# A ConvFFN up-projection computed as seven half-size products per column tile, with the weight sums of the down-projection made earlier in the program

## The chip, the cores and the metric

One core of one Trainium2 chip runs one decoder layer in one launch. The metric is the device time of one execution in microseconds (us), less is better. The kernel before takes 1924.64 us (median of three runs, 1924.29 to 1924.65).

## What is computed

The layer is a sliding-window attention followed by a gated MLP, both with RMSNorms around them, for 512 tokens of width 2048 in float32. The part that matters here:

```python
def conv_ffn(h, w_up, conv_w, w_down):
    u = h @ w_up                                   # (512, 2048) @ (2048, 11264)
    c = conv_w[0] * up[:, 0:S] + ...               # causal, width 3, per column
    gate, val = jnp.split(c, 2, axis=-1)
    return (jax.nn.silu(gate) * val) @ w_down      # (512, 5632) @ (5632, 2048)
```

## The kernel before, in words

**Arithmetic.** Every float32 operand is split into a high and a low half of type fp32r: `split` (L61) lets ScalarE (ACT) write the high half and VectorE (DVE) the difference, and `prod` (L79) issues three matmuls, high by high, high by low, low by high. The activations live as `ah` and `al`, [128 partitions, 4 token blocks, 16 row blocks, 128 tokens]. `weights` (L65) loads a 512 KB weight block into `raw`, and splits it into a pair of a ring of eight (`wh`, `wl`, pool `wsp`).

**Stages.** Attention and its projections; the output projection `oproj` (L466, column groups d = 0 to 3, the last one written out token block by token block); `finish_tok` (L435), which for a token block b makes the residual sum, the RMSNorm, and in `xt` the normalized tokens, that `turn_tok` (L456) transposes on TensorE (PE) into `ah`, `al`; the up-projection; the down-projection.

**Up-projection.** The 11264 columns are handled as 44 column tiles f, each with a gate and a value half of 128 columns. Tiles 0 and 1 are computed in `up_part` (L496) in two sweeps of 256 tokens, since the later tokens come last. For the other 42, `up` (L540) runs `project` (L97) twice: 2 halves by 16 row blocks by 3 matmuls of 512 tokens, 96 matmuls in all. `gate` (L528) then applies convolution, SiLU and product, and its last line stores the tile to DRAM (`hd`, L534).

**Down-projection.** It is already computed with seven instead of eight half-size products (`product`, L608), on 2 token halves (m) by 2 halves of the rows (par). The `hd` parts are read back as four tiles `hq` (m, par); tile (1, 0) lies in a pool of its own (`early`), so that `fetch` (L513) can bring it in while the up-projection runs. The sums of weight blocks that these products need are made by `weight_sums` (L547): one 2 MB load of four blocks by SyncE (SP), four DVE additions (L551), one 2 MB store to a table `td` in DRAM, issued by GpSimd (POOL). It is called after every second tile f, 22 times. `weight_form` (L595) reads blocks from the table or the original weights.

**What sets the order.** The program is written in one stream; a scheduler of the framework places the instructions of ACT, DVE, SP and POOL in a fixed order for each engine. Matmuls keep the order of the program. Each engine runs its list strictly in order, and an instruction that waits holds up all that stand behind it. The same holds for the DMA issues of SP and POOL.

Of the kernel before, what the change touches and what calls it, by code (L numbers as in the profile page):

```python
# [41 lines left out]
def trunk(ctx, tc, xT, x, grow, table, onehot, masked, sinks, conv,  # L42
# [82 lines left out]
    with ExitStack() as att:  # L125
# [10 lines left out]
        with ExitStack() as ph:  # L136
# [26 lines left out]
            for kt in range(KT):  # L163
                if kt == 0:
                    for h in range(2):
                        r = first[:, KT:] if h == 0 else pa.tile([P, 512], F32, name="xs")
                        c = KT + h * S
                        nc.sync.dma_start(r if h else first, xT[:, c if h else 0:c + S])
                        if h == 0:
                            w = [wsp.tile([P, 1024], F32R, name=n) for n in ("wh", "wl")]  # L170
# [243 lines left out]
    hd = dr.tile([2, 2, P, NP, HALF], F32, name="hd")  # L414
    td = dr.tile([NP, P, 4, 1024], F32, name="td")

    with ExitStack() as op:
        acc = op.enter_context(pool("acc", 1, side="right"))
        y = acc.tile([P, NT, D], F32, name="y")
        gp = op.enter_context(pool("gp", 1))  # L420
# [84 lines left out]
        up_part(2)  # L505


    early = ctx.enter_context(pool("early", 1, side="right"))
    fap = ctx.enter_context(pool("fap", 2, side="right"))
    hq = {(1, 0): early.tile([P, NP, HALF], F32, name="hq10")}  # L510
    batches = [(g, min(g + GB, NP)) for g in range(0, NP, GB)]

    def fetch(m, par, g0, g1):  # L513
        nc.sync.dma_start(hq[m, par][:, g0:g1, :], hd[m, par, :, g0:g1, :])  # L514

    with ExitStack() as us:
# [11 lines left out]
        def gate(f, o):  # L528
            cg = conv_half(o[0], f, 0)
            nc.scalar.activation(cg, cg, AF.Silu)  # L530
            cv = conv_half(o[1], f, 1)
            nc.vector.tensor_tensor(cv, cg, cv, ALU.mult)
            kp, par = divmod(f, 2)
            nc.sync.dma_start(hd[:, par, :, kp, :].rearrange("m p t -> p m t"),  # L534
                              cv.rearrange("p (m t) -> p m t", m=2))
            for g0, g1 in batches:
                if par == 0 and kp == g1 - 1:
                    fetch(1, 0, g0, g1)

        def up(f):  # L540
            o = [bank(k) for k in ((0, 1), (2, 5))[f % 2]]
# [5 lines left out]
        def weight_sums(kp):  # L547
            t = tsp.tile([P, 4, 1024], F32, name="ts")
            nc.sync.dma_start(t, wdn[4 * kp:4 * kp + 4].rearrange("q p n -> p q n"))
            for o, a, b in ((2, 0, 2), (0, 0, 1), (1, 2, 1), (3, 1, 3)):  # L550
                nc.vector.tensor_tensor(t[:, o, :], t[:, a, :], t[:, b, :], ALU.add)  # L551
            nc.gpsimd.dma_start(td[kp], t)

        gate(0, o[0:2])
        gate(1, o[2:4])
# [7 lines left out]
    acts.close()  # L563
    acc = ctx.enter_context(pool("acc2", 1))
    y = acc.tile([P, NT, D], F32, name="y")
    g3 = acc.tile([P, D], F32, name="g3")
    rest = ctx.enter_context(pool("rest", 1))
    raws = (wraw, ctx.enter_context(pool("wraw2", 2)))
    for m, par in ((0, 1), (1, 1)):
        hq[m, par] = rest.tile([P, NP, HALF], F32, name=f"hq{m}{par}")  # L570
    small = ctx.enter_context(pool("small3", 4))
    last = ctx.enter_context(ExitStack())
    hq[0, 0] = last.enter_context(pool("hq00", 1)).tile([P, NP, HALF], F32, name="hq00")
# [5 lines left out]
    XB, ZB = (3, 4, 6, 7), (0, 1, 2, 5)  # L579

    def act_form(first, second, sign, g0, g1):
        n = g1 - g0
        a = hq[first][:, g0:g1, :]
        hi = wsp.tile([P, 1024], F32R, name="wh")[:, :n * HALF].rearrange("p (k t) -> p k t", t=HALF)
        lo = wsp.tile([P, 1024], F32R, name="wl")[:, :n * HALF].rearrange("p (k t) -> p k t", t=HALF)
        if second is None:
            nc.scalar.activation(hi, a, AF.Copy, scale=-1.0)
            nc.vector.scalar_tensor_tensor(lo, a, -1.0, hi.bitcast(F32), ALU.mult, ALU.subtract)
        else:
            t = fap.tile([P, GB, HALF], F32, name="fa")[:, :n, :]  # L590
            nc.vector.tensor_tensor(t, a, hq[second][:, g0:g1, :], ALU.subtract if sign < 0 else ALU.add)
            split(hi, lo, t)
        return hi, lo

    def weight_form(src, kp):  # L595
        raw = raws[kp % 2].tile([P, 1024], F32, name="raw")
        table, q = src
        nc.sync.dma_start(raw, td[kp, :, q, :] if table else wdn[4 * kp + q])
        hi = wsp.tile([P, 1024], F32R, name="wh")
        lo = wsp.tile([P, 1024], F32R, name="wl")  # L600
        split(hi, lo, raw)
        return hi, lo

# [152 lines left out]
```

## Time and profile before

| | |
|---|---|
| median of three runs | 1924.64 us |
| profiled execution, its own time | 1924.01 us |
| span in the profile, first to last instruction | 1922.0 us |
| PE busy | 1909.6 us (99%) |
| DVE busy | 1114.5 us (58%) |
| ACT busy | 788.5 us (41%) |
| moved by DMA | 374.78 MB, mean 195 GB/s |

The span is divided by what runs: attention and its projections up to about 373 us, the output projection with `finish_tok` to 528 us, tiles 0 and 1 of the up-projection to 577 us, the other 42 tiles to 1492 us, then the down-projection. "Busy" counts the time in which at least one instruction of the engine is under way; matmuls overlap, so their pace is read from start to start, not from their durations. In lists of instructions a row gives start, duration, engine, line, operation, and in brackets the idle time ahead of it with what ended it.

### The profile page before, as it was taken

How to read it: one execution, taken by the hardware profiler on the slowest of the kernel's cores; microseconds unless marked ns; L12 is line 12 of the kernel's file. 1: busy time of each engine (PE TensorE's matmuls, PEld its weight loads, DVE VectorE, ACT ScalarE, POOL GpSimd, SP SyncE). 2: the span in 40 equal slices, each digit the busy share in tenths (PEclk: the TensorE clock that was granted, in tenths of full speed). 3: DMA queues.
4: the chain of work that ended last, by engine and by line, in shares of the span. 5: the costliest groups of instructions: out<-in, count | busy, mean ns of one | idle time of the engine just before them, and what ended most of it. 6: DMA issues, size and time to landing. Idle time of an engine off the chain costs nothing.

```text
span 1922.0 us, 22964 instructions
## 1 busy us (share of the span) xinstructions
PE 1909.6 (99%) x8846; PEld 1589.2 (83%) x8846; DVE 1114.5 (58%) x1655; ACT 788.5 (41%) x1236; POOL 14.3 (1%) x30
## 2 busy tenths in 40 slices
PE   9999999999999999999999999999999999999998
PEld 7888888888898888888888888888888888888886
DVE  5468888723675555565555533334343476666885
ACT  6357777622443222222222222222222355545553
POOL 0000000000000000000000000000000000000000
PEclk9999999999999999999999999999999999999999
DMA  8623235352367787787778633333332965665773
GB/s 310 149 97 107 92 107 174 135 189 96 119 229 284 286 300 275 283 301 295 285 289 307 234 111 105 121 109 113 118 107 91 352 227 188 195 228 199 246 235 110
DMA packets 105644, 374.78 MB, mean 195 GB/s; under 512 B 10592, under 2 KB 24128, under 8 KB 100800
## 3 DMA queue, kind: packets, MB, share of 16 engines
q1 hardware_dynamic: 98336, 317.98, 48.1%
q0 software_dynamic: 3168, 46.14, 6.5%
q10 hardware_dynamic: 4032, 9.21, 1.5%
q8 instruction: 69, 1.13, 0.2%
q14 instruction: 39, 0.32, 0.1%
HBM read 300.90 MB, written 72.39 MB: 194 GB/s over the span
## 4 chain that ended last, share of the span: by engine, by line
PE 97%; DMA 2%; DVE 0%; ACT 0%; issue 0%; DVEq 0%; SPq 0%; ACTq 0%
PE b L74 96%; PE b L77 2%; DMA hq<-hd 1%; DMA hd<-c 1%; DMA raw<-td 0%; DMA first<-in_xT 0%; DVE x L652 0%; DVE wl L63 0%; ACT wh L62 0%; ACT ah L157 0%; ACT junk L641 0%; DVE y L643 0%; DVEq L752 0%; SPq L514 0%; DVE rs L111 0%
## 5 line engine op out<-in xcount | busy, mean ns | idle before, releaser
L63 DVE TENSOR_TENSOR wl<-raw,wh 128x1024 fp32r<-128x1024 f32 (+1 forms) x411 | 498.5, 1220 | 610.3 <-ACT wh L62 609.4
L62 ACT ACTIVATE wh<-raw 128x1024 fp32r<-128x1024 f32 (+1 forms) x411 | 431.2, 1057 | 818.5 <-PE b L74 675.1
L74 PE MATMUL b<-ah,wh 128*128 128x512 f32 (+1 forms) x1792 | 691.1, 386 | 0.2 <-ACT wh L62 0.2
L74 PE MATMUL b<-ah,wl 128*128 128x512 f32 (+1 forms) x1792 | 684.9, 382 | 0.1
L74 PE MATMUL b<-al,wh 128*128 128x512 f32 (+1 forms) x1792 | 684.0, 382 | 0.0
L74 PEld LDWEIGHTS b<-ah,wl 128*128 128x128 f32 x1792 | 336.8, 188 | 66.0 <-DVE wl L63 0.4
L74 PEld LDWEIGHTS b<-ah,wh 128*128 128x128 f32 x1792 | 337.2, 188 | 63.2 <-ACT wh L62 1.7
L74 PEld LDWEIGHTS b<-al,wh 128*128 128x128 f32 x1792 | 337.3, 188 | 61.5
L74 PE MATMUL b<-wl,wh 128*128 128x512 f32 x616 | 239.8, 389 | 0.8 <-DVE wl L63 0.8
L74 PE MATMUL b<-wh 128*128 128x512 f32 x616 | 239.8, 389 | 0.1
L74 PE MATMUL b<-wh,wl 128*128 128x512 f32 x616 | 239.7, 389 | 0.0
L74 PEld LDWEIGHTS b<-wl,wh 128*128 128x128 f32 x616 | 115.7, 188 | 24.9 <-DVE wl L63 1.1
L74 PEld LDWEIGHTS b<-wh 128*128 128x128 f32 x616 | 115.7, 188 | 24.5 <-ACT wh L62 0.6
L74 PEld LDWEIGHTS b<-wh,wl 128*128 128x128 f32 x616 | 115.7, 188 | 24.0
L74 PE MATMUL b<-wh,ah 128*128 128x512 f32 x320 | 126.5, 395 | 0.0
L74 PE MATMUL b<-wh,al 128*128 128x512 f32 x320 | 124.8, 390 | 0.0
L74 PE MATMUL b<-wl,ah 128*128 128x512 f32 x320 | 124.6, 389 | 0.0
L551 DVE TENSOR_TENSOR ts<-ts 128x1024 f32<-128x1024 f32 x88 | 107.4, 1221 | 27.9 <-DMA ts<-in_wdn 26.7
L524 DVE SCALAR_TENSOR_TENSOR c<-b,cw,c 128x511 f32<-128x511 f32 x88 | 65.4, 744 | 22.9 <-ACT c L523 22.9
L523 ACT ACTIVATE c<-b,cw 128x512 f32<-128x512 f32 x88 | 59.1, 671 | 43.3 <-PE b L74 43.3
L74 PEld LDWEIGHTS b<-wh,al 128*128 128x128 f32 x320 | 60.1, 188 | 12.9
L74 PEld LDWEIGHTS b<-wl,ah 128*128 128x128 f32 x320 | 60.2, 188 | 11.7
(108 smaller groups left out, 1142.9 us busy)
## 6 DMA issues: line engine op xcount, KB each, us to landing
raw<-in_wup SPq DMA_DIRECT2D x176, 512.0 KB, 3.6
ts<-in_wdn SPq DMA_DIRECT2D x22, 2048.0 KB, 8.3
td<-ts POOLq DMA_DIRECT2D x22, 2048.0 KB, 7.8
raw<-td SPq DMA_DIRECT2D x88, 512.0 KB, 4.9
raw<-in_wdn SPq DMA_DIRECT2D x66, 512.0 KB, 4.4
raw<-in_wq SPq DMA_DIRECT2D x32, 512.0 KB, 3.4
raw<-in_wo SPq DMA_DIRECT2D x32, 512.0 KB, 3.4
hd<-c SPq DMA_DIRECT2D x44, 256.0 KB, 3.4
```

The costliest lines, as they stand in the source:

```text
L62: nc.scalar.activation(hi, src, AF.Copy)
L63: nc.vector.tensor_tensor(lo, src, hi.bitcast(F32), ALU.subtract)
L74: tc.keep_in_program_order(nc.tensor.matmul(o, l, r, start=start, stop=stop, skip_group_check=more))
L77: tc.keep_in_program_order(nc.tensor.transpose(o, src, ident))
L523: nc.scalar.activation(c, o, AF.Copy, scale=w[:, 2:3])
L524: nc.vector.scalar_tensor_tensor(c[:, 1:], o[:, :S - 1], w[:, 1:2], c[:, 1:], ALU.mult, ALU.add)
L551: nc.vector.tensor_tensor(t[:, o, :], t[:, a, :], t[:, b, :], ALU.add)
```

## The change

Four things are done.

1. **Seven products.** Tiles f = 4 to 43 go to `up_pair`: gate and value half are taken as two column blocks, the 2048 rows as two row blocks, the 512 tokens as two halves, and the 2 by 2 by 2 product is computed with seven products of 256 tokens by 8 row blocks (Winograd's form). The sums of token blocks are made once, in `token_sums` and `settle`: three forms get tiles of their own, two overwrite quarters of `ah` and `al`, two are quarters as they stand. The sums of weight blocks are made for each tile: four DVE additions, then seven splits in place of four. Partial results are read out of PSUM by four ACT copies (`shot` and one more) and three DVE subtractions of 256 columns. Tile 2 stays as before; tile 3 is computed in two sweeps of 256 tokens (`up_by_tokens`), after each of which a quarter of `ah`, `al` is overwritten.
2. **Weight sums.** `weight_sums` now works block by block on three 512 KB buffers: four loads and four stores of 512 KB, all issued by POOL. Six of its 22 calls stand in the output projection, one ahead of tile 3, fifteen are spread over tiles 5 to 40.
3. **Space.** The ring of weight halves is five instead of eight during the up-projection.
4. **Read-back.** `hq` (1, 0) has no early place any more: all four `hq` tiles are fetched after the up-projection.

```diff
     def weights(dram, u):
...
-        hi = wsp.tile([P, 1024], F32R, name="wh")
-        lo = wsp.tile([P, 1024], F32R, name="wl")
+        hi, lo = halves()
...
+    def weight_sums(kp, sums):
+        def load(q):
+            t = sums.tile([P, 1024], F32, name="ts")
+            nc.gpsimd.dma_start(t, wdn[4 * kp + q])
+            return t
+        def add(q, t, other):
+            nc.vector.tensor_tensor(t, t, other, ALU.add)
+            nc.gpsimd.dma_start(td[kp, :, q, :], t)
+        b11, b21 = load(0), load(2)
+        add(2, b21, b11)
+        b12 = load(1)
+        add(0, b11, b12)
+        add(1, b12, b21)
+        b22 = load(3)
+        add(3, b22, b12)
...
+                if u % 3 == 2:
+                    weight_sums(2 * (d - 1) + u // 3, sums)
...
+                if b < 2 and kt == 8:
+                    weight_sums(4 + b, sums)
...
+        def times(o, n, w, fresh):
+            o3 = o[:, :HALF].rearrange("p (a b) -> p a b", a=2)
+            a = forms[n]
+            for k in range(8):
+                prod(o3, cols(w, k), tuple(v[:, :, k, :] for v in a), fresh and k == 0, k == 7, not fresh)
...
+        def up_pair(f):
+            X, Y, Z = (bank(k) for k in ((0, 1, 6), (3, 4, 7))[f % 2])
...
+            nc.vector.tensor_tensor(t, b11, b21, ALU.add)
+            times(X, 2, form(t), True)
+            s1 = shot(X, "s1")
+            b12 = block(f, 0, 1)
+            times(Z, 7, form(b12), True)
+            s7 = shot(Z, "s7")
+            nc.vector.tensor_tensor(t, t, b12, ALU.add)
+            times(X, 5, form(t), False)
+            s2 = shot(X, "s2")
+            nc.vector.tensor_tensor(b11, b11, b12, ALU.add)
+            times(Z, 6, form(b11), False)
+            b22 = block(f, 1, 1)
+            nc.vector.tensor_tensor(t, t, b22, ALU.add)
+            times(X, 3, form(t), False)
+            s3 = shot(X, "s3")
+            nc.vector.tensor_tensor(ug[:, :HALF], Z[:, :HALF], s2, ALU.subtract)
+            times(Y, 1, form(b21), True)
+            nc.vector.tensor_tensor(uv[:, :HALF], s3, s7, ALU.subtract)
+            times(X, 4, form(b22), False)
+            nc.vector.tensor_tensor(ug[:, HALF:], s1, Y[:, :HALF], ALU.subtract)
+            nc.scalar.activation(uv[:, HALF:], X[:, :HALF], AF.Copy, scale=-1.0)
+            gate(f, (ug, uv))
-        for f in range(2, NF):
-            up(f)
-            if f % 2 == 0:
-                weight_sums(f // 2 - 1)
-        weight_sums(NP - 1)
+        for f in range(4, NF):
+            up_pair(f)
+            if f % 5 in (0, 2) and 7 + 2 * (f // 5 - 1) + (f % 5) // 2 < NP:
+                weight_sums(7 + 2 * (f // 5 - 1) + (f % 5) // 2, sums)
...
-    for q in ((0, 0), (0, 1), (1, 1)):
+    for q in ((1, 0), (0, 0), (0, 1), (1, 1)):
         for g0, g1 in batches:
             fetch(*q, g0, g1)
```

The change moves instructions in three places that the prediction speaks of.

**Place 1, DVE in the up-projection.** Before, one tile f with one set of weight sums (`ts`) in it; `wl` is the low half of a weight block, `c0` and `c1` the convolution, numbers are those of the buffers:

```order
L63 TENSOR_TENSOR wl_7293<-raw_7290,wh_7292 128x1024
L63 TENSOR_TENSOR wl_7323<-raw_7320,wh_7322 128x1024
L524 SCALAR_TENSOR_TENSOR c0_7136<-b0_7014,cw_80,c0_7136 128x511
L525 SCALAR_TENSOR_TENSOR c0_7136<-b0_7014,cw_80,c0_7136 128x510
L551 TENSOR_TENSOR ts_8787<-ts_8787 128x1024 x2
L63 TENSOR_TENSOR wl_7353<-raw_7350,wh_7352 128x1024
L551 TENSOR_TENSOR ts_8787<-ts_8787 128x1024 x2
L63 TENSOR_TENSOR wl_7383<-raw_7380,wh_7382 128x1024
L524 SCALAR_TENSOR_TENSOR c1_7141<-b1_7015,cw_80,c1_7141 128x511
L525 SCALAR_TENSOR_TENSOR c1_7141<-b1_7015,cw_80,c1_7141 128x510
L532 TENSOR_TENSOR c1_7141<-c0_7136,c1_7141 128x512
L63 TENSOR_TENSOR wl_7433<-raw_7430,wh_7432 128x1024
```

Now, from the second addition of one set to its fourth, within one tile of the bunch (`raw` and `bw` are sums of weight blocks and the blocks themselves, `ug`, `uv` the results of a tile):

```order
L433 TENSOR_TENSOR ts_13699<-ts_13699,ts_13705 128x1024
L674 TENSOR_TENSOR raw_9093<-bw_9089,bw_9091 128x1024
L65 TENSOR_TENSOR wl_8922<-raw_8856,wh_8921 128x1024
L433 TENSOR_TENSOR ts_13705<-ts_13705,ts_13701 128x1024
L65 TENSOR_TENSOR wl_8953<-bw_8852,wh_8952 128x1024
L562 SCALAR_TENSOR_TENSOR c1_8825<-uv_8598,cw_83,c1_8825 128x511
L683 TENSOR_TENSOR bw_9089<-bw_9089,bw_9125 128x1024
L562 SCALAR_TENSOR_TENSOR c0_8820<-ug_8597,cw_83,c0_8820 128x511
L686 TENSOR_TENSOR raw_8856<-raw_8856,bw_8980 128x1024
L563 SCALAR_TENSOR_TENSOR c1_8825<-uv_8598,cw_83,c1_8825 128x510
L433 TENSOR_TENSOR ts_13711<-ts_13711,ts_13705 128x1024
L563 SCALAR_TENSOR_TENSOR c0_8820<-ug_8597,cw_83,c0_8820 128x510
```

What moved: the sums of the tile's own blocks (L674 to L686) stand between its splits (L65), and the four additions of a set (L433) are spread between them. The calls are written two in five tiles, but the list has one set in every tile from the fifth on, 54 additions in 14 tiles in a row, and none behind them.

**Place 2, SP at the end of the up-projection.** Before, the last rows that bring in weight blocks for the down-projection (`raw`), the last tiles' stores (`hd`), and the four `hq` (numbered by the buffer: 5346 is (1, 0), 11135 is (0, 1), 11136 is (1, 1), 11143 is (0, 0)):

```order
L598 DMA raw<-td 128x1024 x3
L534 DMA hd<-c_10967 128x2x256
L514 DMA hq_5346<-hd 128x512
L598 DMA raw<-td 128x1024 x2
L514 DMA hq_11135<-hd 128x1024 x5
L514 DMA hq_11136<-hd 128x1024 x4
L534 DMA hd<-c_11108 128x2x256
L514 DMA hq_11136<-hd 128x1024
L598 DMA raw<-td 128x1024 x4
L514 DMA hq_11143<-hd 128x1024 x5
L514 DMA hq_11143<-hd 128x512
L514 DMA hq_11135<-hd 128x512
```

Now (15675 is (0, 0), 15663 is (1, 0), 15667 is (0, 1), 15668 is (1, 1)):

```order
L744 DMA raw<-td 128x1024 x2
L548 DMA hq_15675<-hd 128x1024 x2
L572 DMA hd<-c_15637 128x2x256
L548 DMA hq_15675<-hd 128x1024 x3
L548 DMA hq_15675<-hd 128x512
L548 DMA hq_15663<-hd 128x1024 x5
L548 DMA hq_15663<-hd 128x512
L548 DMA hq_15667<-hd 128x1024 x5
L548 DMA hq_15667<-hd 128x512
L548 DMA hq_15668<-hd 128x1024 x5
L548 DMA hq_15668<-hd 128x512
L744 DMA raw<-td 128x1024 x18
```

What moved: all of `hq` (1, 0) stands behind the store of the very last tile and behind four fetches of (0, 0), and the fifth weight block of the down-projection stands behind all four `hq`.

**Place 3, DVE in `finish_tok` of the first token block.** Before:

```order
L437 TENSOR_REDUCE s_4516<-ssm 128x1
L108 TENSOR_SCALAR rs<-s_4516 128x1
L110 RECIPROCAL rs<-rs 128x1
L111 SCALAR_TENSOR_TENSOR rs<-rs 128x1
L112 TENSOR_SCALAR rs<-rs 128x1
L113 TENSOR_TENSOR s_4516<-rs 128x1
L444 SCALAR_TENSOR_TENSOR y<-y,s_4516,xt 128x1024 x2
L447 TENSOR_TENSOR s_4527<-s_4527 128x1
L108 TENSOR_SCALAR rs<-s_4527 128x1
```

Now:

```order
L465 TENSOR_REDUCE s_4602<-ssm 128x1
L433 TENSOR_TENSOR ts<-ts 128x1024
L117 TENSOR_SCALAR rs<-s_4602 128x1
L119 RECIPROCAL rs<-rs 128x1
L433 TENSOR_TENSOR ts<-ts 128x1024
L120 SCALAR_TENSOR_TENSOR rs<-rs 128x1
L433 TENSOR_TENSOR ts<-ts 128x1024
L121 TENSOR_SCALAR rs<-rs 128x1
L122 TENSOR_TENSOR s_4602<-rs 128x1
L472 SCALAR_TENSOR_TENSOR y<-y,s_4602,xt 128x1024 x2
L475 TENSOR_TENSOR s_4613<-s_4613 128x1
L117 TENSOR_SCALAR rs<-s_4613 128x1
```

What moved: three additions of a set of weight sums (L433) stand ahead of the residual sum (L472), and behind these rows a fourth stands ahead of the normalized tokens `xt`.

## Rows read from the trace of the kernel before

**Rows 1.** The page, chain that ended last: shares of the span by engine.

```profile
PE 97%; DMA 2%; DVE 0%; ACT 0%; issue 0%; DVEq 0%; SPq 0%; ACTq 0%
```

**Rows 2.** Busy times by stretch: start:end, length, PE, PEld, DVE, ACT, POOL, PEclk, DMA, GB/s.

```profile
577.00:1493.00 916.00, 916.00 (x4047) 758.91 (x4046) 451.06 (x464) 255.88 (x298) 11.18 (x21) 1.00 0.59 211
1493.00:1922.00 429.00, 418.52 (x1845) 345.79 (x1843) 287.22 (x284) 210.00 (x238) 0.00 (x0) 0.99 0.65 221
1905.00:1922.00 17.00, 7.41 (x33) 5.82 (x31) 9.02 (x21) 2.47 (x8) 0.00 (x0) 0.85 0.33 123
```

**Rows 3.** PE's waits, whole span: sum in us, times, longest.

```profile
PE b L74 <- DVE zero L140: 1.5, 1, 1.5
PE b L74 <- DVE wl L63: 0.8, 1, 0.8
```

**Rows 4.** Timeline of PE from 640 us, 512 columns: first and last of 90 matmuls.

```profile
639.67 0.39 PE L74 MATMUL b<-ah,wl 128*128 128x512 f32 x1
...
659.84 0.39 PE L74 MATMUL b<-al,wh 128*128 128x512 f32 x1
```

**Rows 5.** Timeline of PE from 560 us, 256 columns: first and last of 144 matmuls.

```profile
559.75 0.28 PE L74 MATMUL b<-al,wh 128*128 128x256 f32 x1
...
576.91 0.28 PE L74 MATMUL b<-ah,wh 128*128 128x256 f32 x1
```

**Rows 6.** Timeline of DVE, a stretch in which it runs without idle time.

```profile
568.92 1.22 DVE L63 TENSOR_TENSOR wl<-raw,wh 128x1024 fp32r<-128x1024 f32 x1
570.06 0.74 DVE L524 SCALAR_TENSOR_TENSOR c<-b,cw,c 128x511 f32<-128x511 f32 x1
570.72 1.21 DVE L551 TENSOR_TENSOR ts<-ts 128x1024 f32<-128x1024 f32 x1
571.85 0.74 DVE L525 SCALAR_TENSOR_TENSOR c<-b,cw,c 128x510 f32<-128x510 f32 x1
...
574.30 0.68 DVE L532 TENSOR_TENSOR c<-c,c 128x512 f32<-128x512 f32 x1
574.90 1.22 DVE L63 TENSOR_TENSOR wl<-raw,wh 128x1024 fp32r<-128x1024 f32 x1
```

**Rows 7.** Groups of instructions by line and shape: the nearest to a 256-column subtraction.

```profile
L217 DVE TENSOR_TENSOR vs<-qn,vs 128x256 fp32r<-128x256 f32 x8 | 2.9, 416 | 0.0
```

**Rows 8.** Timeline of DVE and POOL, last addition of two sets and their stores.

```profile
572.61 0.67 POOL L552 DMA_DIRECT2D td<-ts  x1 [569.57 <-DVE c L525]
...
596.05 1.22 DVE L551 TENSOR_TENSOR ts<-ts 128x1024 f32<-128x1024 f32 x1
...
597.58 0.53 POOL L552 DMA_DIRECT2D td<-ts  x1 [24.30 <-DVE ts L551]
```

**Rows 9.** DMA issues from 600 to 1050 us: count, KB each, median us to landing.

```profile
DMA packets 30997, 130.58 MB, mean 290 GB/s; under 512 B 2336, under 2 KB 7712, under 8 KB 28576
...
raw<-in_wup SPq DMA_DIRECT2D x84, 512.0 KB, 5.5
...
hq<-hd SPq DMA_DIRECT2D x3, 512.0 KB, 3.9
```

**Rows 10.** The same from 1120 to 1480 us, where no weight sums are made.

```profile
DMA packets 14469, 40.24 MB, mean 112 GB/s; under 512 B 1360, under 2 KB 5712, under 8 KB 14452
...
raw<-in_wup SPq DMA_DIRECT2D x59, 512.0 KB, 3.4
```

**Rows 11.** Timeline of DVE and PE, end of finish_tok for the first token block.

```profile
500.54 2.74 DVE L451 SCALAR_TENSOR_TENSOR xt<-y,s,g 128x512 f32<-128x512 f32 x4
...
504.99 0.60 PE L77 MATMUL b<-ident,xt 128*128 128x128 f32 x4
```

**Rows 12.** Timeline of SP and ACT at the start of the down-projection.

```profile
1492.13 7.22 SPq L514 DMA_DIRECT2D hq<-hd  x9
...
1514.23 1.06 ACT L62 ACTIVATE wh<-raw 128x1024 fp32r<-128x1024 f32 x1 [0.24 <-DMA raw<-td]
...
1515.52 1.06 ACT L62 ACTIVATE wh<-raw 128x1024 fp32r<-128x1024 f32 x1 [0.23 <-DMA raw<-td]
```

More of the change, by code (lines that the diff above doesn't have):

```diff
@@ L53, in trunk @@
     act = acts.enter_context(pool("act", 1))
+    more = acts.enter_context(ExitStack())
+    ring = {"slots": [wsp] * 5 + [more.enter_context(pool("wsp2", 3))] * 3, "next": 0}
     def bank(i):
@@ L63, in split, with halves, ring_of @@
         nc.vector.tensor_tensor(lo, src, hi.bitcast(F32), ALU.subtract)
+    def halves():
+        p = ring["slots"][ring["next"] % len(ring["slots"])]
+        ring["next"] += 1
+        return p.tile([P, 1024], F32R, name="wh"), p.tile([P, 1024], F32R, name="wl")
+    def ring_of(*slots):
+        ring["slots"], ring["next"] = [p for p, n in slots for _ in range(n)], 0
     def weights(dram, u):
@@ L169, in trunk @@
                         if h == 0:
-                            w = [wsp.tile([P, 1024], F32R, name=n) for n in ("wh", "wl")]
+                            w = halves()
                             raw = wraw.tile([P, 1024], F32, name="raw")
@@ L505, in trunk @@
         up_part(2)
-    early = ctx.enter_context(pool("early", 1, side="right"))
-    fap = ctx.enter_context(pool("fap", 2, side="right"))
-    hq = {(1, 0): early.tile([P, NP, HALF], F32, name="hq10")}
+    more.close()
+    ring_of((wsp, 5))
     batches = [(g, min(g + GB, NP)) for g in range(0, NP, GB)]
+    hq = {}
     def fetch(m, par, g0, g1):
-        nc.sync.dma_start(hq[m, par][:, g0:g1, :], hd[m, par, :, g0:g1, :])
+        t, k0 = next((t, k) for t, k, k1 in hq[m, par] if k <= g0 < k1)
+        nc.sync.dma_start(t[:, g0 - k0:g1 - k0, :], hd[m, par, :, g0:g1, :])
     with ExitStack() as us:
-        cp = us.enter_context(pool("cp", 3, side="right"))
-        tsp = us.enter_context(pool("tsp", 1, side="right"))
+        fp = us.enter_context(pool("fp", 1))
+        cp = us.enter_context(pool("cp", 2))
+        sums = us.enter_context(pool("tsu", 3))
+        held = us.enter_context(ExitStack())
+        keepers = held.enter_context(pool("tk", 1, side="right"))
+        temps = us.enter_context(ExitStack())
         def conv_half(o, f, half):
@@ L545, in up, with up_by_tokens @@
             gate(f, o)
[L547 to L552, printed above, removed]
+        def up_by_tokens(f):
+            o = [bank(k) for k in (2, 5)]
+            w = {(h, u): weights(wup, 4 * f + 2 * h + u) for h in range(2) for u in range(2)}
+            for m in range(2):
+                for h in range(2):
+                    o3 = o[h].rearrange("p (a b) -> p a b", a=NT)[:, 2 * m:2 * m + 2, :]
+                    for kt in range(KT):
+                        prod(o3, cols(w[h, kt // 8], kt % 8), moving(kt, 2 * m, 2 * m + 2), kt == 0, kt == KT - 1)
+                n = (7, 1)[m]
+                for c in range(2):
+                    k = slice(4 * c, 4 * c + 4)
+                    settle(n, kept[n][:, :, k, :], k, (-1.0, 1.0)[m])
+            gate(f, o)
@@ L554, in trunk, with block @@
         gate(0, o[0:2])
+        token_sums(0)
         gate(1, o[2:4])
-        for f in range(2, NF):
-            up(f)
-            if f % 2 == 0:
-                weight_sums(f // 2 - 1)
-        weight_sums(NP - 1)
+        token_sums(1)
+        up(2)
+        temps.close()
+        bw = us.enter_context(pool("bw", 6))
+        weight_sums(6, sums)
+        up_by_tokens(3)
+        held.close()
+        un = us.enter_context(pool("un", 2, side="right"))
+        def block(f, r, c):
+            t = bw.tile([P, 1024], F32, name="bw")
+            nc.sync.dma_start(t, wup[4 * f + 2 * c + r])
+            return t
@@ new lines, in form, with shot @@
+        def form(t):
+            w = halves()
+            split(*w, t)
+            return w
+        def times(o, n, w, fresh):
[3 more added lines that the diff above has]
+                prod(o3, cols(w, k), tuple(v[:, :, k, :] for v in a), fresh and k == 0, k == 7, not fresh)
+        def shot(o, name):
+            t = un.tile([P, HALF], F32, name=name)
+            nc.scalar.activation(t, o[:, :HALF], AF.Copy)
+            return t
@@ new lines, in up_pair @@
+        def up_pair(f):
+            X, Y, Z = (bank(k) for k in ((0, 1, 6), (3, 4, 7))[f % 2])
+            ug = un.tile([P, S], F32, name="ug")
+            uv = un.tile([P, S], F32, name="uv")
+            b11, b21 = block(f, 0, 0), block(f, 1, 0)
+            t = wraw.tile([P, 1024], F32, name="raw")
+            nc.vector.tensor_tensor(t, b11, b21, ALU.add)
[20 more added lines that the diff above has]
+            gate(f, (ug, uv))
@@ L579, in trunk, with part @@
     XB, ZB = (3, 4, 6, 7), (0, 1, 2, 5)
+    def part(q, g0, g1):
+        t, k0 = next((t, k) for t, k, k1 in hq[q] if k <= g0 < k1)
+        return t[:, g0 - k0:g1 - k0, :]
     def act_form(first, second, sign, g0, g1):
         n = g1 - g0
-        a = hq[first][:, g0:g1, :]
-        hi = wsp.tile([P, 1024], F32R, name="wh")[:, :n * HALF].rearrange("p (k t) -> p k t", t=HALF)
-        lo = wsp.tile([P, 1024], F32R, name="wl")[:, :n * HALF].rearrange("p (k t) -> p k t", t=HALF)
+        a = part(first, g0, g1)
+        hi, lo = (v[:, :n * HALF].rearrange("p (k t) -> p k t", t=HALF) for v in halves())
         if second is None:
@@ L590, in act_form @@
             t = fap.tile([P, GB, HALF], F32, name="fa")[:, :n, :]
-            nc.vector.tensor_tensor(t, a, hq[second][:, g0:g1, :], ALU.subtract if sign < 0 else ALU.add)
+            nc.vector.tensor_tensor(t, a, part(second, g0, g1), ALU.subtract if sign < 0 else ALU.add)
             split(hi, lo, t)
@@ L598, in weight_form @@
         nc.sync.dma_start(raw, td[kp, :, q, :] if table else wdn[4 * kp + q])
-        hi = wsp.tile([P, 1024], F32R, name="wh")
-        lo = wsp.tile([P, 1024], F32R, name="wl")
+        hi, lo = halves()
         split(hi, lo, raw)
```

50 lines of the change are left out of this document (43 added, 7 removed).

## The prediction

> **What bounds the kernel now.** I read the chain that ended last first: PE has 97% of it [rows 1]. Then the stretches. From 577 to 1493 us, tiles 2 to 43 of the up-projection, PE is busy in all 916 us, DVE in 451, ACT in 256, at full clock; in the down-projection it is busy in 418.5 of 429 [rows 2]. PE's waits are small, the longest 1.5 us in attention and 0.8 us on a low weight half (`wl`) [rows 3]. So the time is PE's pace, and half of DVE is free. The rest is priced from that pace, and from DVE's, since DVE gets the new work.
>
> **PE.** In dense stretches 512-column matmuls start every (659.84 − 639.67) / 89 = 0.2266 us [rows 4], 256-column ones every (576.91 − 559.75) / 143 = 0.1200 us [rows 5]; both paces include a weight load for each matmul. Half the columns thus cost 53% of the time, so that seven half-size products don't save an eighth: a tile goes from 96 × 0.2266 = 21.76 to 168 × 0.1200 = 20.16 us, −1.6. Forty tiles: **−63.8 us**. Tile 3, 192 × 0.1200 = 23.04: **+1.3**. The reads of PSUM between products (`shot`) cost PE nothing, since a product on another bank (24 matmuls, 2.9 us) stands ahead of the next use of the same bank, against 0.4 us of a 256-column operation [rows 7]. ACT gets seven splits of 1.06 [rows 12], four copies and the gate: some 11 us a tile, hidden.
>
> **DVE in the up-projection.** Back to back, a 1024-element operation takes 1.14 us of DVE (568.92 to 570.06), a convolution step 0.66, a product of 512 0.60 [rows 6]; for a 256-column subtraction I take the 0.4 of [rows 7] (at least 0.3, half of the 512). A new tile has 7 splits and 4 block sums: 11 × 1.14 + 4 × 0.66 + 0.6 + 3 × 0.4 = 17.0 us, under 20.16, PE bounds. With a set of weight sums it has 15 × 1.14 + 4.4 = 21.5, and DVE bounds. The order of place 1 has a set in each of 14 tiles in a row: 14 × (21.5 − 20.16) = **+18.8**.
>
> To this come waits for the sets' blocks. With three buffers, the fourth block's load waits for the store behind the set's second addition (`add(0)`), and its fourth addition waits for that load; the third block of the next set waits in the same way for the fourth addition's store; POOL issues both. A hop is an addition's end to POOL's issue, 597.58 − 597.27 = 0.31 [rows 8], the landing, and 0.2 to go on. The landing of a 512 KB transfer by POOL is in no row. Bounds: 3.4 us in a quiet stretch (112 GB/s) [rows 10]; 5.5 for `raw` at 290 GB/s, about what a new tile moves too (twelve transfers of 512 KB in 21.5 us), but beside lumps of 2 MB; in that same stretch, `hq` of 512 KB took 3.9 [rows 9]. I take 3.9, since the lumps go. Two hops are then 8.8, against 8.8 us of DVE work (6 × 1.14 + 3 × 0.66) between the additions on one side, 10.05 on the other: nearly covered, **+4** for the stage (3.4: 0; 5.5: +72). At the start, DVE also makes the token sums and their halves, 4 × 2.3 + 22 × 1.14 = 34 us, within the 65 us of tiles 1 to 3, where the first sets stand as well: **+3** (0 to 15). Together **+26** (14 with the small subtraction, no wait and no start; 94 with landing 5.5).
>
> Does POOL wait for DVE? Of the 22 store issues on POOL, 21 took 0.53 to 0.54 us, and one, at 572.61 in a stretch where DVE never pauses, 0.67 [rows 8]: no sign that POOL waits for DVE. The Trainium skill, "GPSIMD Engine Reference", § 1 Specifications, says that GpSimd and VectorE share SBUF interfaces and contend when DVE's instruction has two SBUF inputs; by that, each issue could wait out a running addition. It is a rival below.
>
> **Start of the down-projection.** Before, four batches of `hq` and the weight blocks needed were on hand; PE lost 0.8 us at most [rows 3]. Now (place 2) SP stands at the store of the last tile. That comes after a copy, two convolution steps, SiLU and product of tile 43, five operations of 0.4 to 0.75 us and four hand-overs of 0.31 [rows 6 to 8]: 4.5 us after the last matmul. Behind it come 3.5 batches of (0, 0), 16.5 batches of the three others, the store itself (half a batch) and the fifth weight block, 21.5 in all. Where the queue is full, 512 KB land every 1.30 us (splits at 1514.23 and 1515.52, each released by its transfer) [rows 12]: 28 us. With 3.4 − 1.3 = 2.1 for the first landing and 2.6 for the split (1.06 + 0.31 + 1.2), the fifth block is ready 37 us after the last matmul. In the meantime PE has the first four blocks, 48 × 0.2266 = 10.9. Lost: 37 − 10.9 − 0.8 = **+25**. At least 18, if the tail and the split are hidden (−7).
>
> At the other end the clock counts: where PE was busy in 7.41 of 17 us, the granted clock was 0.85 [rows 2], so a stretch like this one is not all at 2.4 GHz. Were the four blocks computed at 1.2 GHz, they would take 21.8 and still end inside the wait; what comes after it may lose 3.4, so 29. The Trainium skill, "TensorE: Matmul & The Clock Gate", Part 1, says that an idle array falls to 1.2 GHz; by it the 29 would stand.
>
> **`finish_tok` of the first block.** Four additions (place 3) stand ahead of `xt`: 4 × 1.14 = 4.6, against a slack of 504.99 − 501.2 (first of the four `xt` done) = 3.8 before PE's transposes [rows 11]: 0.8. With two hops of wait, +8.6. I take **+4**, the middle. The other sets in the output projection lie where DVE idles, and cost nothing.
>
> **Sum.** −63.8 + 1.3 + 26 + 25 + 4 = −7.5 against the profiled execution's 1924.01 (span 1922.0): 1916.5. The median of the runs is 0.6 above it: **1917 us**. About 0.2%, 3.85 us, is what a measurement of this kernel can tell from no change.
>
> **Rivals.**
> - *The ring of three buffers bounds the bunched tiles (slower).* With landing 5.5, as `raw` in [rows 9], two hops are 12.0; DVE stalls 3.2 + 1.95 in each of 14 tiles, 72 us: 1985. It decides from a landing of 4.3, where the gain is gone; 5.0 gives 1956. For it: the mean traffic is the same. Against: no 2 MB lumps, and 3.9 in the same stretch. With what lies between 4.3 and 5.5: chance 0.25.
> - *POOL waits for DVE at each issue (slower).* 0.57 to 1.14 us an issue make two hops longer by 1.1 to 2.3, the stage by 13 to 46: 1930 to 1963. The rule of the Trainium skill, "GPSIMD Engine Reference", § 1, would do this. The 0.53 us speak against: 0.05.
> - *The small costs vanish (faster).* Bunch 14, transition 18, `finish_tok` 0.8: −29.7, 1895. For it: each is a wait in a chain that may overlap. 0.17.
> - *No change to tell*: landing 4.1 to 4.4, or a transition and a start at their upper ends, 1921 to 1928. 0.18.
> - *The change doesn't do what it says.* "Spread" is written two sets in five tiles, which would put DVE at 18.8 on average, under 20.16, and make the bunch cost nothing. The order speaks against it; were the waits to hold the sets back so that they spread, the time falls to the faster rival's.
> - My forecast, 1905 to 1921: 0.33. Other slower mishaps: 0.02.
>
> **How the numbers follow.** Faster 0.33 + 0.17 = 0.50, same 0.18, slower 0.25 + 0.05 + 0.02 = 0.32. The range 1893 to 1955 takes the faster rival in, and of the ring's rival the part up to landing 5.0; left out are some 0.03 below and 0.14 above. The forecast's own range is 1905 to 1921.
>
> **What would show it.** Right: in the profile after, the quiet tiles take 20.2 us and the bunched ones 21.5 to 22, with DVE over 95% busy there; after the last matmul of tile 43, PE idles some 25 us on `hq` or `raw`; POOL's loads land in 3.7 to 4.2 us. Wrong: DVE's additions (L433) idle on loads for over 1 us a tile, or PE's pace with 256 columns differs from 0.120, or the idle time at the transition is under 15 us.

## The result, and the profile after

The kernel after the change takes 1970.89 us (median of four runs, 1968.34 to 1972.94) against 1924.64 (by now four runs, 1924.29 to 1925.05): slower, ratio 1.024, 95% interval 1.0222 to 1.0257. The forecast was 1917 with a range of 1893 to 1955; the time lies outside it, 54 us above the forecast. The profiled execution has a span of 1971.2 us, 49.2 more than before.

The span can be cut at matmuls that are the same before and after, counted in the list of PE's instructions (each tile of the new kind is 168 matmuls, of the old kind 96; PE keeps the order of the program):

| stretch | before, us | after, us | difference | forecast |
|---|---|---|---|---|
| up to the first matmul of tile 2 | 578.0 | 604.9 | +26.9 | +4 |
| tiles 2 and 3 | 43.5 | 44.8 | +1.3 | +1.3 |
| tiles 4 to 18 (15 tiles) | 326.4 | 359.4 | +33.0 | +2 (26 − 15 × 1.6) |
| tiles 19 to 43 (25 tiles) | 544.0 | 504.0 | −40.0 | −39.9 |
| from there to the end | 430.1 | 458.1 | +28.0 | +25 |

So the products themselves gave what was forecast, 20.16 us a tile, in the 25 tiles without weight sums. The loss stands in three places. The windows of these places, with the same columns as in [rows 2]:

```profile
484.00:530.00 46.00, 25.19 (x97) 19.49 (x96) 23.02 (x36) 9.89 (x22) 8.53 (x16) 0.81 0.68 243
...
675.50:1009.10 333.60, 300.38 (x2354) 295.34 (x2353) 299.23 (x323) 145.02 (x210) 55.59 (x104) 0.95 0.77 266
...
1009.10:1513.10 504.00, 504.00 (x4202) 503.98 (x4200) 424.77 (x470) 265.24 (x372) 0.00 (x0) 1.00 0.37 116
1513.10:1555.00 41.90, 16.78 (x57) 12.53 (x56) 15.20 (x16) 11.63 (x14) 0.00 (x0) 0.70 0.92 354
```

In `finish_tok` PE works 25 of 46 us; in tiles 5 to 18 (the second row) it is idle for 33 us; at the start of the down-projection it works 17 of 42. Before, PE was busy in all of the up-projection [rows 2]. The chain that ended last, 97% PE in [rows 1], now passes through DMAs, DVE and "issue":

```profile
PE 73%; DMA 12%; issue 8%; DVE 6%; POOL 1%; ACT 0%; SPq 0%; DVEq 0%; POOLq 0%; ACTq 0%
```

The four largest of PE's waits over the whole span answer to [rows 3], where the longest but one was 0.8 us:

```profile
PE b L83 <- DVE wl L65: 41.7, 21, 5.9
PE b L83 <- ACT wh L64: 24.0, 4, 17.4
PE b L86 <- ACT rs L118: 12.0, 1, 12.0
PE b L83 <- ACT s L665: 5.0, 5, 2.0
```

**Tiles 5 to 18.** They take 333.6 us, 23.8 each. DVE is busy 299.2 / 14 = 21.4 us a tile, as forecast (21.5); the rest of a tile, 2.5 us, it stands idle. DVE's waits in this stretch:

```profile
DVE ts L433 <- DMA ts<-in_wdn: 15.1, 11, 2.9
DVE ts L433 <- issue: 14.4, 8, 2.8
DVE raw L674 <- DMA bw<-in_wup: 1.7, 1, 1.7
```

Some 30 of its 34 idle microseconds stand ahead of additions of the weight sums (L433). The forecast had 4. The landings in the stretch from 690 to 1000 us, which answer to [rows 9]:

```profile
bw<-in_wup SPq DMA_DIRECT2D x52, 512.0 KB, 6.1
td<-ts POOLq DMA_DIRECT2D x51, 512.0 KB, 4.4
ts<-in_wdn POOLq DMA_DIRECT2D x49, 512.0 KB, 6.4
```

A store and the load behind it take 4.4 + 6.4 = 10.8 us, where the forecast took 2 × 3.9 = 7.8.

**`finish_tok` of the first block.** DVE, POOL and PE; a row's bracket is the idle time ahead of it:

```profile
508.45 0.54 POOL L434 DMA_DIRECT2D td<-ts  x1 [6.12 <-DVE ts L433]
509.07 0.53 POOL L429 DMA_DIRECT2D ts<-in_wdn  x1
...
514.50 1.23 DVE L433 TENSOR_TENSOR ts<-ts 128x1024 f32<-128x1024 f32 x1 [5.79 <-DMA ts<-in_wdn]
...
519.68 2.48 DVE L472 SCALAR_TENSOR_TENSOR y<-y,s,xt 128x1024 f32<-128x1024 f32 x2
...
526.48 1.23 DVE L433 TENSOR_TENSOR ts<-ts 128x1024 f32<-128x1024 f32 x1 [2.32 <-DMA ts<-in_wdn]
...
528.79 2.74 DVE L479 SCALAR_TENSOR_TENSOR xt<-y,s,g 128x512 f32<-128x512 f32 x4
...
529.64 1.08 PE L86 MATMUL b<-ident,xt 128*128 128x128 f32 x4 [12.00 <-ACT rs L118]
```

An addition waits 5.8 us for a block whose load (509.07) stood behind a store (508.45), and the small steps of the norm stand behind it in DVE's list; another addition stands ahead of `xt`. The transposes start 24.65 us later than in [rows 11]. PE had lost some 9 us before that, on weight halves that stood behind such additions.

**Start of the down-projection.** SP's queue, in place of [rows 12]:

```profile
1501.15 0.80 SPq L744 DMA_DIRECT2D raw<-td  x2
1516.48 0.80 SPq L548 DMA_DIRECT2D hq<-hd  x2
1517.38 0.37 SPq L572 DMA_DIRECT2D hd<-c  x1
1517.80 22.15 SPq L548 DMA_DIRECT2D hq<-hd  x22
```

The last matmul of tile 43 starts at 1513.00. SP stands from 1502 to 1516.5 at two fetches of (0, 0), whose space is not free until a convolution step of the last tile; everything else is behind them. PE waits 17.4 us for the first batch of (1, 0) and 2.0 for a low weight half, then, after four weight blocks, 5.3 and 0.5 us for the fifth: 25.1 us in all, called the gaps at the transition below (0.9 before).

### The profile page after: what moved, and what is told of

Its sections match the earlier page's. It is cut to its first block, busy times and chain, and to the rows that moved or that the text cites. A ratio compares the mean times of both kernels' runs of the same rounds, so it can differ in the third digit from the quotient of the medians.

```text
span 1971.2 us, 30073 instructions
## 1 busy us (share of the span) xinstructions
PE 1877.9 (95%) x11822; PEld 1701.0 (86%) x11822; DVE 1492.2 (76%) x2079; ACT 979.8 (50%) x1566; POOL 96.6 (5%) x184
## 4 chain that ended last, share of the span: by engine, by line
PE 73%; DMA 12%; issue 8%; DVE 6%; POOL 1%; ACT 0%; SPq 0%; DVEq 0%; POOLq 0%; ACTq 0%
PE b L83 71%; DMA td<-ts 5%; DMA ts<-in_wdn 4%; DVE wl L65 2%; PE b L86 2%; DVE ts L433 2%; DMA raw<-in_wo 1%; DMA hq<-hd 1%; POOL td L434 1%; POOL ts L429 0%; DMA raw<-td 0%; DMA bw<-in_wup 0%; DVE c L562 0%; DVE bw L683 0%; ACT wh L64 0%
## 5 line engine op out<-in xcount | busy, mean ns | idle before, releaser
L64 ACT ACTIVATE wh<-raw 128x1024 fp32r<-128x1024 f32 (+1 forms) x371 | 388.3, 1055 | 490.6 <-PE b L83 255.3
L65 DVE TENSOR_TENSOR wl<-raw,wh 128x1024 fp32r<-128x1024 f32 (+1 forms) x371 | 449.1, 1219 | 215.1 <-ACT wh L64 214.5
L83 PE MATMUL b<-ah,wl 128*128 128x256 f32 (+1 forms) x1824 | 563.2, 309 | 28.3 <-DVE wl L65 28.3
L83 PE MATMUL b<-ah,wh 128*128 128x256 f32 (+1 forms) x1824 | 568.3, 312 | 5.6 <-ACT s L665 4.3
L83 PE MATMUL b<-al,wh 128*128 128x256 f32 (+1 forms) x1824 | 560.1, 307 | 0.4 <-DVE al L65 0.4
L83 PEld LDWEIGHTS b<-ah,wh 128*128 128x128 f32 x1824 | 355.7, 195 | 19.2 <-ACT s L665 5.1
L64 ACT ACTIVATE wh<-bw 128x1024 fp32r<-128x1024 f32 x160 | 167.7, 1055 | 116.4 <-PE b L83 116.3
L65 DVE TENSOR_TENSOR wl<-bw,wh 128x1024 fp32r<-128x1024 f32 x160 | 194.3, 1220 | 9.8 <-ACT wh L64 9.4
L433 DVE TENSOR_TENSOR ts<-ts 128x1024 f32<-128x1024 f32 x88 | 107.4, 1221 | 91.1 <-DMA ts<-in_wdn 65.1
L83 PEld LDWEIGHTS b<-wh,wl 128*128 128x128 f32 x616 | 116.7, 189 | 24.2
L665 ACT ACTIVATE s<-b 128x256 f32<-128x256 f32 x160 | 59.4, 372 | 108.0 <-PE b L83 107.7
L83 PE MATMUL b<-f5h,wl 128*128 128x256 f32 x320 | 90.7, 283 | 1.4 <-DVE wl L65 1.4
```

The costliest lines, as they stand in the source:

```text
L83: tc.keep_in_program_order(nc.tensor.matmul(o, l, r, start=start, stop=stop, skip_group_check=more))
L433: nc.vector.tensor_tensor(t, t, other, ALU.add)
L665: nc.scalar.activation(t, o[:, :HALF], AF.Copy)
```

## The experiments

Three causes were to be told from their rivals: waits through the three buffers (against DVE's work, the traffic, or POOL's queue), the sets in the output projection, and the order of the read-back. Lines are those of the changed kernel. "Loss in the tiles" is the time of tiles 4 to 43, up to the end of the last matmul, over 40 × 20.16 us; after the change it is 57.0 (tile 4 alone 5.6). x9 changes the kernel before, all others the kernel after; runs of before beside them had medians of 1924.43 to 1927.18. x1 to x6 were run once each. The kernels run four times or more spread over 2 to 5 us, x8 over 16.

**x1: no additions.**

```diff
         def add(q, t, other):
-            nc.vector.tensor_tensor(t, t, other, ALU.add)
             nc.gpsimd.dma_start(td[kp, :, q, :], t)
```

> The four additions of each set are left out (the table gets the blocks themselves); loads and stores by POOL stay. Theory (DVE stands in order behind additions that wait for a store and a load through three buffers): DVE waits for no block any more, so tiles 4 to 18 fall from 24.0 us a tile to 20.2 to 20.5, the start of the second tile's sweep and finish_tok go back to within 3 us of before, and the 28 us at the start of the down-projection stay: 1885 to 1897 us. Rival (the traffic of the sums slows the up-projection's own blocks, which land in 6.1 us in that stretch): the tiles stay above 22 us, 1915 us or more.

Measured: 1891.05 us. The loss in the tiles is 2.0 us, tile 2 starts at 578.63 (before: 577.99), and 25.0 us of gaps stay at the transition. PE's waits:

```profile
PE b L83 <- ACT wh L64: 22.2, 2, 18.0
PE b L83 <- DVE wl L65: 2.7, 2, 2.0
```

All transfers of the sums were there, with 282 GB/s from 645 to 928 us against 266 in tiles 5 to 18 after the change, so traffic alone costs PE nothing; the loss goes with what DVE has to do and to wait for.

**x2: the two sets in the last column group moved to the up-projection.**

```diff
-                if b < 2 and kt == 8:
-                    weight_sums(4 + b, sums)
...
             up_pair(f)
+            if f in (38, 41):
+                weight_sums(4 + (f - 38) // 3, sums)
```

> The two sets that are called inside the last column group of the output projection move to the up-projection (called after tiles 38 and 41). Theory (finish_tok of the first token block waits for their blocks): the 26 us by which tile 2 starts later than before fall to under 4, two more sets cost 3.8 us each in the bunch, 1971 - 23 + 8 = 1956 us (1950 to 1961). Rival (the four sets of column groups 1 and 2 do it, since additions stand ahead of weight halves there too): about 10 us of the 26 stay, 1966 us.

Measured: 1973.5 us, no gain. Tile 2 starts at 585.63, 8 us later than before instead of 27; so 19 of the 27 go with the two sets, 8 with the four others. But the loss in the tiles rises from 57.0 to 76.7, 10 us for each set that was moved, where 3.8 was expected: the scheduler makes the bunch longer (8 us are lost in tiles 19 and 20), and tiles 4 to 18 lose 12 us more. Neither expected time was met; each had half of the place right.

**x3: one ring for the tile's blocks and the sets' blocks.**

```diff
-        sums = us.enter_context(pool("tsu", 3))
...
-        bw = us.enter_context(pool("bw", 6))
+        bw = us.enter_context(pool("bw", 9))
...
-                weight_sums(7 + 2 * (f // 5 - 1) + (f % 5) // 2, sums)
+                weight_sums(7 + 2 * (f // 5 - 1) + (f % 5) // 2, bw, "bw")
```

> The blocks of the sums take turns in one ring of nine buffers with the tile's own blocks, instead of three of their own, so that a set cannot be loaded ahead of its place and the order of DVE has two sets in five tiles up to tile 39. Theory (the bunch, one set a tile through three buffers, is the loss): DVE has 18.7 us of work a tile on average and PE sets the pace; the 57 us of tiles 4 to 18 fall to 5 to 15 over all tiles, 1920 to 1932 us. Rival one (each set costs its wait wherever it stands, 2.5 us, and its 1.2 us of work): about 57 us stay, spread, 1965 to 1975 us. Rival two (traffic): the tiles with a set stay above 22 us.

Measured: 1927.0 us, as expected by the theory. The loss in the tiles is 9.1, 7.2 of it in tile 4, where the last token halves are made (x1 loses 1.8 there, with no addition). Space is the same, work is the same. The order differs, since a set can no longer be loaded before its tile's turn; but so does the ring, since a set's blocks no longer follow one another through three buffers. This run doesn't tell the two apart; x5, next but one, has another ring and keeps the bunch.

**x4: part (1, 0) of the read-back in the space of forms 5 and 6.**

```diff
+    fk = ctx.enter_context(pool("fk", 1, side="right"))
...
+            if f == NF - 1:
+                for g0, g1 in batches:
+                    fetch(1, 0, g0, g1)
             times(X, 3, form(t), False)
...
-    hq[1, 0] = [(rest.tile([P, NP, HALF], F32, name="hq10"), 0, NP)]
```

> Part (1, 0) of the read-back goes into the space of forms 5 and 6, which the last tile is done with 8 us before its end, and is fetched from there on; the other three follow behind five more weight blocks. Nothing else is changed. Theory (PE waits because (1, 0), the first that it needs, is queued behind the last store and four pieces of (0, 0)): of the 28 us lost there 3 to 8 stay, 1971 - 22 = 1948 us (1945 to 1953). Rival (the queue is full, 11.5 MB at about 400 GB/s, and PE waits for that whatever the order): 20 us or more stay, 1963 us or more.

Measured: 1963.36 us, outside the theory's numbers, but the place answers to it: the gaps at the transition fall from 25.1 to 7.9 us. From the end of tile 43 to the end it is 440.5 us (458.1 after, 430.1 before), so that 10 of the 28 us stay, near the theory's 3 to 8 and far from the rival's 20. The other 8 us were lost earlier: tile 2 starts 2.9 us later than after the change, and the loss in the tiles rises to 62.0, where the scheduler laid out the bunch anew. SP's queue:

```profile
1509.71 0.79 SPq L548 DMA_DIRECT2D f5h<-hd  x2
1510.55 1.14 SPq L548 DMA_DIRECT2D f5l<-hd  x2
1511.80 0.48 SPq L548 DMA_DIRECT2D f6h<-hd  x1
```

The batches start 11 us before the last matmul (1520.9 here). Most of the loss was the order in the queue, not its length.

**x5: four buffers.**

```diff
-        sums = op.enter_context(pool("tso", 3))
+        sums = op.enter_context(pool("tso", 4))
...
-        cp = us.enter_context(pool("cp", 2))
-        sums = us.enter_context(pool("tsu", 3))
+        cp = us.enter_context(pool("cp", 1))
+        sums = us.enter_context(pool("tsu", 4))
```

> The sets get four buffers of their own instead of three, in the output projection and in the up-projection (the convolution's tiles go from two buffers to one for the space). The bunch in DVE's order stays, one set a tile in a dozen tiles. Theory (the store and the load that follow one another in the same buffer make DVE wait; a set of four blocks needs that twice with three buffers, once with four): in the bunch DVE's work of 21.4 us a tile sets the pace, its waits for blocks fall from 34 to under 10 us, and the 58 us of loss over 20.16 us a tile to 25 to 33; the loss in finish_tok falls to under 12: 1920 to 1935 us. Rival (transfers of POOL's queue are slow, 6.4 us for a load, and every set waits for them with any number of buffers): over 45 us stay in the tiles, 1955 us or more.

Measured: 1938.6 us. The loss ahead of tile 2 is gone but for 0.8 us (578.82; the transposes start at 505.16, before 504.99), more than expected. The loss in the tiles is 46.8, above the theory's 33. DVE's waits from 678.4 to 933 us, eleven tiles of the bunch:

```profile
DVE raw L674 <- DMA bw<-in_wup: 19.3, 9, 3.0
DVE ts L433 <- DMA ts<-in_wdn: 1.7, 1, 1.7
```

The wait for the sets' blocks is gone with the fourth buffer, so the ring was its cause; a wait for the tile's own blocks, 1.7 us in the same place after the change, has taken its place. With a set in every tile DVE has some 21.2 us of work a tile, and SP's loads of these blocks stand waiting for DVE to give buffers back (209 of 255 us); they land in 6.1 us, as after the change. That this is why they come late is argued, not tried; one of the two buffers of the convolution's tiles also went.

**x6: loads by SP.**

```diff
-            nc.gpsimd.dma_start(t, wdn[4 * kp + q])
+            nc.sync.dma_start(t, wdn[4 * kp + q])
```

> The four loads of a set are issued by SP instead of POOL; stores stay with POOL, three buffers stay. Theory (ring of three: store, then load, whichever queue issues them): a load lands perhaps 1 us sooner, but a store and a load still follow one another, so 40 us or more of the 58 us of loss in the tiles stay, 1950 to 1975 us. Rival (POOL's one queue is the cause, where a load stands behind stores and waits of the same queue): the loss in the tiles falls to 25 to 30 us, the bare work of the bunch, and the time to 1925 to 1940 us.

Measured: 1969.72 us, within what the theory expected; the loss in the tiles is 62.4. Tile 2 starts at 593.05, 12 us sooner than after the change; tiles 2 and 3 lose 3 of that, the other tiles 5. Landings from 666 to 983 us:

```profile
td<-ts POOLq DMA_DIRECT2D x50, 512.0 KB, 5.0
ts<-in_wdn SPq DMA_DIRECT2D x49, 512.0 KB, 4.7
```

The loads land 1.7 us sooner than by POOL, the stores 0.6 later. That store and load follow one another counts, not which queue issues them. Why the tiles did not gain even the 1.1 us of the sum stays open; SP issues these loads in one list with the tile's own.

**x7 and x8: the cures together.** x7 has x3's ring with 18 sets evenly after tiles 5 to 39, x4's read-back, and four sets in column groups 1 and 2 of the output projection. In x8 all 22 sets stand in the up-projection, and the last three parts are fetched one batch after each weight block:

```diff
                 wf = weight_form(src, kp)
+                if kp > 2 and queue:
+                    fetch(*queue.pop(0))
```

> Three cures together: sets from the blocks' ring of nine, 18 of them evenly after tiles 5 to 39, none ahead of tile 3; four in column groups 1 and 2 of the output projection and none in the last; read-back part (1, 0) fetched early. From 1927 of the ring alone: 18 less at the start of the down-projection, 19 less in finish_tok, 7 less in tile 4, up to 5 more for three more sets: 1880 to 1893 us. If the losses only move (each cure showed its gain beside the others' losses, and the up-projection now has DVE at 94%), 1900 us or more.

> As the one before, but with no set in the output projection: all 22 stand in the up-projection, and the three other read-back parts are fetched one batch at a time between the weight blocks of the first product. Theory (the four sets in column groups 1 and 2 still delay tile 2 by 7 us; DVE has 19.5 us of work a tile against 20.16): tile 2 starts where it did before, within 1 us, the start of the down-projection loses under 4 us, the tiles lose up to 12 in all: 1868 to 1885 us. Rival (at 97% DVE no longer keeps ahead of PE, for any wait of a set then delays PE): the tiles lose 20 us or more and it is slower than the version with four sets ahead.

Measured: x7 1879.85 us (ratio to before 0.9765, 0.9749 to 0.9781), a little better than expected: the loss in the tiles is 1.6, the gaps at the transition 9.5, tile 2 starts at 586.00. x8 1907.5 us (1903.42 to 1919.20; 0.9921, 0.9895 to 0.9947): tile 2 starts at 579.07 and the gaps at the transition are 2.3, both about as the theory had it, but the loss in the tiles is 47.3, the rival's case. DVE's waits from 645 to 1380 us of x8:

```profile
DVE raw L671 <- DMA bw<-in_wup: 32.7, 18, 4.8
DVE bw L433 <- DMA bw<-in_wdn: 10.5, 9, 2.2
```

With 18 sets in 40 tiles DVE has 17.0 + 0.45 × 4.56 = 19.1 us a tile, with 22 it has 19.5, both under 20.16. But it is not the mean alone that tells: x7 never has a set in two tiles in a row, x8 does at eight places, each tile with 21.5 us of DVE work, and 44 of the 47.3 us are lost in the second tile of such a pair or the one behind it. More than 20 sets can't stand in 40 tiles without such pairs; whether the 3% that 22 sets leave would be enough without them was not tried.

**x9: the sums alone, in the kernel before.** The block-by-block `weight_sums` with three buffers is put into the kernel before; its calls stay. Line numbers in the rows are those of this kernel.

> The kernel before with one part of the change alone: its 22 calls of the weight sums work block by block through three buffers of 512 KB, loads and stores by POOL, where they stood. Its order of DVE, too, has one set a tile, in tiles 3 to 20. Theory (the waits cost only where DVE's work fills the tile): a tile has 4 splits, 4 additions and the convolution, 12.4 us of 21.76, so that 4 to 9 us of waits for blocks fit beside it, and eight pairs of weight halves lie ahead of PE: within 4 us of before, 1921 to 1929 us. Rival (an order in which splits stand behind additions that wait holds PE up with any amount of free time, as in finish_tok): 10 us or more slower.

Measured: 1961.72 us, ratio 1.0193 (1.0179 to 1.0207): the rival's case, and far beyond it. DVE has hardly more than half of a tile's time in work there, and twelve tiles of the bunch (10 to 21) still take 24.9 us in place of 21.8; the tiles ahead of them lose nothing yet. PE's waits there, and rows of DVE, POOL and PE in one of these tiles:

```profile
PE b L74 <- DVE c L525: 25.0, 7, 7.3
...
855.05 1.22 DVE L554 TENSOR_TENSOR ts<-ts 128x1024 f32<-128x1024 f32 x1 [6.54 <-DMA ts<-in_wdn]
...
857.30 0.53 POOL L550 DMA_DIRECT2D ts<-in_wdn  x1
...
860.83 0.54 POOL L550 DMA_DIRECT2D ts<-in_wdn  x1 [3.00 <-DMA td<-ts]
...
864.82 1.22 DVE L554 TENSOR_TENSOR ts<-ts 128x1024 f32<-128x1024 f32 x1 [5.61 <-issue]
865.97 0.74 DVE L525 SCALAR_TENSOR_TENSOR c<-b,cw,c 128x510 f32<-128x510 f32 x1
...
866.85 0.77 PE L74 MATMUL b<-ah,wh 128*128 128x512 f32 x1 [7.03 <-DVE c L525]
```

A convolution step stands in DVE's list behind an addition that waits 5.6 us; PE needs the bank that the step reads, and waits 7.0. This settles more than it was meant to: DVE need not be full for the bunch to be dear. One set through three buffers has a cycle of two stores, two loads, two additions and the hand-overs. By the medians of the landings, 4.4 and 6.4 us after the change and 3.6 and 6.4 here, that is an estimated 24 to 26 us. Measured, a set of four additions came every 25.7 us in tiles 5 to 18 after the change and every 22.1 in tiles 10 to 21 here. There the order had 52 additions in 14 tiles, here 54 in 12: 0.93 and 1.13 sets a tile, which gives the 23.8 and 24.9 us that a tile took. An order with about one set a tile ties the tiles to that cycle.

**x10: the best version.** x7 with four buffers for the sets of the output projection (as in x5) and x8's order of fetches.

> The version with spread sets and the early read-back, and two more cures: four buffers for the sets in the output projection, and the three later read-back parts fetched one batch at a time between the weight blocks of the first product. Theory (each took its loss away where it was tried): tile 2 starts where it did before (7 us less), the start of the down-projection loses 2 us in place of 10: 1879.9 - 15 = 1865 us (1861 to 1871). Rival (the two losses shift, since the order of DVE or SP changes elsewhere): 1873 us or more.

Measured: 1864.85 us (1863.91 to 1866.30), ratio 0.9687 (0.9674 to 0.9701), 60 us under the kernel before and 106 under the change. Tile 2 starts at 578.40, the loss in the tiles is 1.8, the gaps at the transition 2.5, and all of PE's waits are these:

```profile
PE b L83 <- DVE zero L149: 1.5, 1, 1.5
PE b L83 <- ACT s L664: 1.3, 1, 1.3
PE b L83 <- ACT uv L696: 1.3, 1, 1.3
PE b L83 <- DVE wl L65: 1.2, 3, 0.5
```

## Why the prediction was wrong

In spans the forecast misses by some 57 us: 31 in tiles 4 to 18, 23 ahead of tile 2, 3 at the start of the down-projection.

- **PE: right.** 20.16 us a tile and 23.04 for tile 3, from the 0.1200 us pitch of [rows 5]. In the 25 tiles without sets it held to the hundredth.
- **DVE's work in the bunch: right as a size, wrong as the bound.** 21.4 us a tile against 21.5. It gives 17 of the 51.4 us that tiles 5 to 18 lost. The rest are waits, and x9 shows that such a bunch costs 3 us a tile even where DVE has time to spare.
- **The waits for blocks: the step that failed.** "I take 3.9, since the lumps go" for the landing: stores landed in 4.4 and loads in 6.4. The row that was set aside, `raw` with 5.5 at the same traffic [rows 9], was the better one: the mean of 4.4 and 6.4 is 5.4. With the text's own hand-overs of 1.0 us a store and its load took 11.8 us against 8.8 and 10.05 of DVE work beside them, and DVE waited 2.5 us a tile, 34 in all, where 4 were taken; 2.2 of the 2.5 stand ahead of additions, which the text had named as a sign of being wrong. The mechanism itself stood in the text as the first rival, with 1985 us at a landing of 5.5 and the turn at 4.3. It had a chance of 0.25, and the range was cut at a landing of 5.0. Its formula gives waits of 4.75 us a tile at the measured landings, more than came: 13 sets stood in these 14 tiles, so that 23.0 us of DVE work lay beside each, against the 25.7 that a set took.
- **`finish_tok`: wrong by size.** +4 was the middle between a bare slack and one pair of waits; 27 came ahead of tile 2. By then the sets run behind their places: eight of the thirteen additions from 461 us on wait, by up to 7.1 us, not the last alone (x2: 19 us by the two sets called there; x5: all but 0.8 gone with a fourth buffer). "The other sets in the output projection lie where DVE idles, and cost nothing" is wrong by 8 us (x2): DVE's idle time lay ahead of a split, and the additions' waits now lie there.
- **Start of the down-projection: right in sum, not in order.** +25 forecast, +28.0 measured. The text had PE compute four weight blocks first and wait then; it waited 17.4 us first, for (1, 0), which the first product needs, and 5.3 later, so that the sum was met in part by luck. That the full queue sets it fell with x4 and x8: in the right order the same bytes leave gaps of 2.3 us. The gaps grew by 24.2 of the 28.0; the other 4 us go with the clock, 0.70 in that window and 0.50 from 1530.6 to 1534.0 us, close to the 3.4 that the forecast allowed. The Trainium skill, "TensorE: Matmul & The Clock Gate", Part 1, lets the clock fall on an idle array, and the trace agrees.
- **POOL and DVE.** POOL's issues took 0.53 to 0.55 us in the stretch where DVE was busy 90% of the time, as in [rows 8], so POOL's issues do not wait for DVE. The Trainium skill, "GPSIMD Engine Reference", § 1 Specifications, speaks of a contention there; the trace shows none for issues of DMAs. Whether DVE lengthens a transfer of POOL behind its issue no run separates; loads by SP landed 1.7 us sooner, and the tiles gained nothing (x6).
- **"The change doesn't do what it says"** was nearer than its place among the rivals. The sums written as spread were bunched by the scheduler; truly spread (x3, in another ring), they cost 9 us instead of 57.

## What to carry to other kernels

Price a chain through a small ring of buffers by its whole cycle, each store and load with the landing of the nearest row at the same traffic, and set it beside the time in which the engine's order wants one turn of it; free time of the engine does not help when others stand behind the waiting instruction in the same list. Where a scheduler sets the order, buffers are the means to hold it: a ring shared with the work of the tile kept the sets at their places, and three buffers of their own let them run ahead. At a change of stage, look at what each engine needs first and put exactly that first in the queue.

## What was not expected of the hardware

- In tiles 5 to 18 PE was idle 22 times, for 0.3 to 4.2 us at a time, and still the granted clock was 0.95 there: PE was busy for 300.4 us with matmuls that take 14 × 20.16 = 282.2 at 2.4 GHz, 18 us more. Whether this cost time where DVE set the pace was not tried. In x9, where DVE is half idle, 25.2 of the 37 us lost are PE's waits and some 11 are matmuls that follow one another more slowly, at a granted clock of 0.97 from 600 to 1000 us.
- Of two transfers of equal size, by the same queue and in the same stretch, the loads took 2 us longer than the stores (6.4 against 4.4 us). By SP, loads took 4.7 (x6). Of the 49 loads of POOL, the 21 that were issued within 0.8 us of POOL's issue ahead took 7.0 us (median) and the other 28 took 5.9, so that going out right behind a store is a part of it at most. The direction alone was not tried.
